# Transposing the second half's x among the first half's products, and keeping its columns in DRAM

## The chip, the cores and the metric

The kernel runs on one core of one Trainium2 chip. The metric is the device time of one execution in microseconds (us), lower is better. The core has five engines that run side by side, each with its own fixed queue of instructions: TensorE (PE, matmuls and transposes; PEld are its weight loads), VectorE (DVE), ScalarE (ACT), GpSimd (POOL) and SyncE (SP, which here only issues DMAs; ACT issues some too).

## The reference, cut to what matters

Two layers over x of 2048 positions by 1024 channels, in float32. Each first forms u from x by a scale and a shift per channel, multiplies u by a wide weight, mixes over time, multiplies by an output weight and normalises:

```python
cond = jax.nn.silu(c)
for l in range(DEPTH):
    shift, scale, gate = ...          # from cond @ ada_w[l] + ada_b[l]
    u = x * (1.0 + scale) + shift
    # l == 0: [a | g | z] = u W_in + b_in; h = a * sigmoid(g); h = causal depthwise conv of 31 taps;
    #         h = swish(LayerNorm(h)); y = (h * silu(z)) W_out + b_out
    # l == 1: [B | C | v | z] = u W_in; y = (B * conv_3(C * v) * silu(z)) W_out
    x = LayerNorm(ALPHA * x + gate * y)
```

## The kernel before

The positions are treated in two halves (`sc` 0 and 1), and each half as its even and odd positions (`hf`). A layer's input product of a half is a list of pairs of 128-column blocks of the weight (12 pairs in layer 0, names `wa`, `wz`). Each pair is computed with seven block products (a seven-product scheme for a 2 by 2 block product) instead of eight, so that seven tiles of u per block of 256 channels are needed: `b11`, `b21`, `t1`, `t2`, `b22`, `t3`, `t4`. Each of them is split in a high part (a cast on ACT) and a low part (a subtraction on POOL or DVE), and one product is 12 matmuls of 128 by 512: high times high, high times low, low times high, for four blocks of channels.

u is needed with channels on the partitions, and x has positions there. `u_block` therefore loads a block of x (`xk`, 128x4x128, two buffers), `u_columns` transposes it on PE into a PSUM bank (`ptx`, tag "tp", two banks that the statistics of the convolution use as well) and applies scale and shift on ACT into a tile `uf` (six buffers). `u_first` and `u_second` then make the seven tiles of one block of channels.

The first half's weights are split as they are used, into five buffers `wa`/`wz`, and each split weight is stored in DRAM (`kepta`, `keptz`, 512 KB each, issued on ACT's queue after the next evacuation) for the second half to load. A weight buffer is free again when its store has landed.

The depthwise convolution of 31 taps runs on DVE (L555, one instruction for each tap; the accumulators are `pca`, `pcb`, `pcd`). It is cut into steps, and `tick` hands out some of them after each product: 3.2 in the body of the first half, 1 in the products listed in `moves`, which are the last eleven of the first half. Among these eleven the generator `second_u` makes the seven u tiles of the second half, in the buffers that the first half's tiles leave.

A scheduler lays out each engine's queue from this program order, from priorities (evacuations and u tiles are urgent, taps are not) and from its own estimate of times. PE's instructions keep the program's order. The names in the profile: `ua0..` and `ua1..` are u tiles of the first and second half, `ufua` is `uf`, `c11`, `c12`, `c22`, `c21` are evacuated products, `pl` the transposes for the statistics.

Of the kernel before, what the change touches and what calls it, by code (L numbers as in the profile page):

```python
# [16 lines left out]
P = 128  # L17
D = 1024
S = 2048
K = D // P  # L20
KH = K // 2
T = 512
# [17 lines left out]
def hybrid_trunk(ctx, tc, x, c, ada_w, ada_b, a_w_in, a_b_in, a_conv_w, a_conv_b,  # L40
# [7 lines left out]
    nc = tc.nc  # L48
# [7 lines left out]
    def st(tag, shape, name, dtype=F32):  # L56
        return sb.tile(shape, dtype, tag=tag, bufs=BUFS[tag], name=name)
# [22 lines left out]
    def store_late(dst, src, then=None):  # L80
        late.append((dst, src, then))
# [30 lines left out]
    def tick(taps, *gens):  # L112
        clock[0] += 1
        due_taps[0] += taps
        conv_steps(int(due_taps[0]))
        due_taps[0] -= int(due_taps[0])
        for gen in gens:
            next(gen, None)
        due = [job for at, job in waiting if at <= clock[0]]
        waiting[:] = [w for w in waiting if w[0] > clock[0]]  # L120
        for job in due:
            job()
# [99 lines left out]
    def u_tile(src, name, eng=None):  # L222
        hi = st("u", [P, T], name + "h", F32R)
        lo = st("u", [P, T], name + "l", F32R)
        split(src, hi, lo, eng)
        return hi, lo
# [12 lines left out]
    def u_block(src, sc, hf, k, su, bu, name, tag):  # L239

        xk = st(tag, [P, NT, P], f"xk{name}{hf}_{k}")
        load(xk, quarters(src)[sc, hf][:, k * P:(k + 1) * P]
             .rearrange("(t p) j -> p t j", p=P), "u")
        return u_columns(xk, hf, k, su, bu, name)
# [6 lines left out]
    def u_second(U, f0, f1, name):  # L251
        (b11, b21), (b12, b22) = f0, f1
        tt = lambda o, a, b: nc.vector.tensor_tensor(o, a, b, op=ALU.subtract)
        with urgent():
            tt(b11, b12, b11)
            U["t1"].append(u_tile(b11, name + "t1", nc.vector))
            U["b22"].append(u_tile(b22, name + "b22"))
            tt(b11, b22, b11)
            U["t2"].append(u_tile(b11, name + "t2"))
            tt(b12, b22, b12)  # L260
            U["t3"].append(u_tile(b12, name + "t3"))
            t4 = st("uf", [P, T], f"{name}t4")
            tt(t4, b21, b11)
            U["t4"].append(u_tile(t4, name + "t4", nc.vector))
# [731 lines left out]
    def slowly(gen, ticks=2):  # L996
        due = 0
        for _ in gen:
            due += ticks
            while due >= 1:  # L1000
                yield
                due -= 1
# [18 lines left out]
    def background_b():  # L1021
# [6 lines left out]
        for h in range(2):  # L1028
            for _ in fold_gate(1, h, b_w_out[0], res[1, 2, h]):
                yield  # L1030
                yield
                yield

    def second_u():

        for i in range(KH):
            f0, f1 = [], []
            for b in range(2):
                for hf, fs in ((0, f0), (1, f1)):
                    fs.append(u_block(x, 1, hf, 2 * i + b, su0, bu0, "ua1", "xk"))  # L1040
                    if hf == 0 or b == 0:
                        yield
            u_parts(US[0, 1], f0, f1, f"ua1{i}")
            yield
# [6 lines left out]
    head = [(0, 6)]  # L1051
    order_a = [at for at in head + order_of(n_a) if at not in early]
    coming = second_u()
    for n, (p, r) in enumerate(order_a):
        product(pa[0][p], r)
        if n < K:
            zero_window(n)
        for n in range(moves.get((p, r), 0)):
            next(coming)
        if (p, r) in ((late_b, 3), (late_a, 4)):  # L1060
            k = 0 if r == 3 else 1
            product(pa[1][0], 1, [k])
            product(pa[1][0], 2, [k])
        queue_convs()
        tick(1 if (p, r) in moves else RATE["a"])
    flush()
    product(pa[1][0], 5, [0, 1])
    product(pa[1][1], 1, [0, 1])
# [130 lines left out]
```

## Time and profile before

| | |
|---|---|
| median of 3 runs | 1720.44 us (1716.67 to 1728.08) |
| the profiled execution, its own time | 1725.78 us |
| its span from first to last instruction | 1724.0 us |
| mean granted TensorE clock | 0.96 of full speed |
| PE busy | 1578.9 us, 92% of the span |
| DVE busy | 1165.1 us, 68% |
| POOL busy | 956.8 us, 56% |
| ACT busy | 665.9 us, 39% |

The shares are means over stages with different limits. The products of layer 0's first half lie between about 105 and 378 us of the span, those of the second half from there to about 615 us.

### The profile page before, as it was taken

The numbers are of one execution on the slowest core, as the hardware profiler recorded it, in microseconds if no ns is written. First come the engines' busy times: TensorE is split into PE (matmuls) and PEld (weight loads), VectorE is DVE, ScalarE is ACT, GpSimd is POOL, SyncE is SP. The second block draws the span as 40 slices with busy tenths as digits, with TensorE's granted clock in tenths as the row PEclk, the third lists the DMA queues.
The fourth block names the chain that finished last, engine by engine and source line by source line (L and its number), as shares of the span: only waits on it lengthen the run. The fifth ranks groups of instructions, "written<-read, shape, count | busy, mean of one in ns | idle before, by whom it ended". The sixth has DMA issues, their size and how long they took to land.

```text
span 1724.0 us, 20944 instructions
## 1 busy us (share of the span) xinstructions
PE 1578.9 (92%) x6860; PEld 1278.1 (74%) x6860; DVE 1165.1 (68%) x1816; ACT 665.9 (39%) x1134; POOL 956.8 (56%) x808
## 2 busy tenths in 40 slices
PE   4699999889999989868999999898899999999996
PEld 3577787668888767656777887677688888878885
DVE  4438999997899887997999963564832222226555
ACT  2345444655533335373444333333732221112221
POOL 4368886965656343866888776727565541121110
PEclk9799999899999989988999999899899999999998
DMA  7358888779999997634777667986688887787995
GB/s 221 114 198 295 293 298 322 228 276 391 333 354 363 357 368 257 208 147 166 265 266 255 245 245 286 342 289 223 220 294 282 306 298 221 229 299 260 329 336 222
DMA packets 237916, 469.64 MB, mean 272 GB/s; under 512 B 20328, under 2 KB 102640, under 8 KB 237808
## 3 DMA queue, kind: packets, MB, share of 16 engines
q1 hardware_dynamic: 190864, 323.06, 55.6%
q10 hardware_dynamic: 46944, 145.25, 21.7%
q8 instruction: 55, 0.90, 0.2%
q14 instruction: 53, 0.43, 0.1%
HBM read 297.72 MB, written 170.52 MB: 272 GB/s over the span
## 4 chain that ended last, share of the span: by engine, by line
PE 59%; DVE 18%; DMA 11%; issue 4%; POOL 3%; ACT 3%; SPq 1%; ACTq 0%; DVEq 0%; POOLq 0%
PE po L98 17%; PE pxb L98 7%; PE pxc L98 7%; PE pxa L98 5%; PE pzb L98 4%; DVE pca L555 4%; PE pzc L98 4%; PE pza L98 3%; DVE pcb L555 3%; DMA keptb<-wb 3%; PE pxz L98 2%; DMA wr<-w_dram 2%; DMA kepta<-wa 2%; PE pya L98 2%; PE pyb L98 2%
## 5 line engine op out<-in xcount | busy, mean ns | idle before, releaser
L555 DVE SCALAR_TENSOR_TENSOR pcb<-h,w,pcb 128x512 f32<-128x512 f32 x224 | 166.7, 744 | 8.4 <-ACT pcb L563 8.0
L555 DVE SCALAR_TENSOR_TENSOR pca<-h,w,pca 128x512 f32<-128x512 f32 x192 | 142.8, 744 | 0.2
L555 DVE SCALAR_TENSOR_TENSOR pca<-xs,w,pca 128x512 f32<-128x512 f32 x128 | 95.5, 746 | 0.8
L825 DVE TENSOR_TENSOR r<-po,r 128x512 f32<-128x512 f32 x64 | 43.3, 683 | 70.0 <-PE po L98 31.6
L555 DVE SCALAR_TENSOR_TENSOR pcd<-xs,w,pcd 128x512 f32<-128x512 f32 x112 | 83.4, 745 | 0.1
L500 POOL TENSOR_TENSOR ada<-ada,adaw 128x512 f32<-128x512 f32 x48 | 63.9, 1331 | 35.1 <-ACT adaw L494 16.0
L795 ACT ACTIVATE r<-r,nb,rs 128x512 f32<-128x512 f32 x64 | 47.3, 808 | 80.4 <-DVE nb L792 80.3
L220 POOL TENSOR_TENSOR gb_0l<-vb,gb_0h 128x512 fp32r<-128x512 f32 x4 | 5.2, 1295 | 110.2 <-ACT gb_0h L219 110.2
L530 POOL TENSOR_TENSOR wf<-wf,grow 128x512 f32<-128x512 f32 x32 | 41.9, 1318 | 37.6 <-DMA wf<-in_b_w_out_dram 33.6
L832 POOL TENSOR_TENSOR rs<-rs,mhalf 128x1 f32<-128x1 f32 x32 | 18.3, 584 | 75.6 <-DVE rs L831 75.6
L220 POOL TENSOR_TENSOR wa<-rawa,wa 128x512 fp32r<-128x512 f32 x32 | 43.2, 1352 | 21.2 <-ACT wa L219 21.0
L569 POOL TENSOR_TENSOR lead<-lead,part 128x512 f32<-128x512 f32 x32 | 43.6, 1362 | 19.8 <-ACT part L568 17.3
L220 POOL TENSOR_TENSOR wc<-rawc,wc 128x512 fp32r<-128x512 f32 x32 | 46.0, 1437 | 15.5 <-ACT wc L219 15.3
L894 POOL TENSOR_TENSOR hb1c<-c12c,c22c 128x512 f32<-128x512 f32 x16 | 21.1, 1322 | 59.1 <-DVE c22c L392 54.8
L220 POOL TENSOR_TENSOR wf<-wf 128x512 fp32r<-128x512 f32 x32 | 43.0, 1351 | 18.4 <-ACT wf L219 13.7
L804 DVE TENSOR_TENSOR r<-r,g 128x512 f32<-128x512 f32 x48 | 39.6, 838 | 20.0 <-PE ptx L101 17.5
L786 POOL TENSOR_TENSOR r<-r,gb 128x512 f32<-128x512 f32 x32 | 43.9, 1388 | 15.7 <-DMA r<-in_x_dram 14.4
L817 ACT ACTIVATE ub<-ptx,post_sh,post_sc 128x128 f32<-128x128 f32 x128 | 47.0, 482 | 13.4 <-PE ptx L101 13.4
L494 ACT ACTIVATE adaw<-adaw,cond 128x512 f32<-128x512 f32 x64 | 42.5, 715 | 24.8 <-DMA adaw<-in_ada_w_dram 24.3
L220 POOL TENSOR_TENSOR wb<-rawb,wb 128x512 fp32r<-128x512 f32 x32 | 45.2, 1412 | 7.6 <-ACT wb L219 7.4
L220 POOL TENSOR_TENSOR wb<-sb,wb 128x512 fp32r<-128x512 f32 x24 | 35.4, 1473 | 25.0 <-ACT wb L219 25.0
L739 ACT ACTIVATE v<-v,second_columns 128x512 f32<-128x512 f32 x32 | 25.9, 814 | 55.0 <-DVE v L738 53.8
(1388 smaller groups left out, 5589.2 us busy)
## 6 DMA issues: line engine op xcount, KB each, us to landing
wr<-w_dram SPq DMA_DIRECT2D x128, 512.0 KB
kepta<-wa ACTq DMA_DIRECT2D x56, 512.0 KB
wa<-kepta SPq DMA_DIRECT2D x56, 512.0 KB
keptc<-wc ACTq DMA_DIRECT2D x56, 512.0 KB
keptb<-wb ACTq DMA_DIRECT2D x56, 512.0 KB
wc<-keptc SPq DMA_DIRECT2D x56, 512.0 KB
wb<-keptb SPq DMA_DIRECT2D x56, 512.0 KB
adaw<-in_ada_w_dram SPq DMA_DIRECT2D x32, 512.0 KB
```

What stands on the lines that cost most here:

```text
L98: return tc.keep_in_program_order(nc.tensor.matmul(*args, **kw))
L220: (eng or nc.gpsimd).tensor_tensor(lo, src, hi.bitcast(F32), op=ALU.subtract)
L494: nc.scalar.activation(raw[:, j], raw[:, j], AF.Identity, scale=cond[:, kk + j:kk + j + 1])
L500: nc.gpsimd.tensor_tensor(acc, acc, raw[:, j], op=ALU.add)
L530: nc.gpsimd.tensor_tensor(w[:, 1], w[:, 1], grow, op=ALU.mult)
L555: nc.vector.scalar_tensor_tensor(out=tiles[out], in0=src, scalar=w, in1=tiles[acc], op0=ALU.mult, op1=op)
L569: nc.gpsimd.tensor_tensor(lead, lead, part, op=ALU.add)
L786: nc.gpsimd.tensor_tensor(rt, rt, gb[0][h], op=ALU.add)
L795: nc.scalar.activation(rts[t, h], rts[t, h], AF.Identity, scale=rs, bias=nb)
L804: eng.tensor_tensor(r, r, g[h], op=ALU.mult)
L817: nc.scalar.activation(fs[k][:, t * P:(t + 1) * P], pt[:, j * P:(j + 1) * P], AF.Identity, scale=post_sc[:, k:k + 1], bias=post_sh[:, k:k ...
L825: nc.vector.tensor_tensor(r, pss[t], r, op=ALU.add)
```

## The change

The sixteen blocks of the second half's x are loaded, transposed, scaled and shifted early, one block after every fourth product of the first half (`columns_early`), and each resulting tile is stored in DRAM (`ux_dram`, 256 KB, on ACT's queue). `second_u` then loads these tiles (`ux`) instead of making them. In the eleven products of `moves` no steps of the convolution are handed out any more, where there was one for each. The low part of `t2` is computed on DVE instead of POOL for the second half.

```diff
-            U["t2"].append(u_tile(b11, name + "t2"))
+            U["t2"].append(u_tile(b11, name + "t2", nc.gpsimd if name < "ua1" else nc.vector))
...
+    ux_dram = dt_([2, K, P, T], "ux_dram")
+
+    def columns_early():
+
+        for k in range(K):
+            for hf in range(2):
+                f = u_block(x, 1, hf, k, su0, bu0, "ua1", "xk")
+                store_late(ux_dram[hf, k], f)
+                yield
+
     def second_u():
...
-                    fs.append(u_block(x, 1, hf, 2 * i + b, su0, bu0, "ua1", "xk"))
+                    k = 2 * i + b
+                    f = st("uf", [P, T], f"ux{hf}_{k}")
+                    load(f, ux_dram[hf, k], "u")
+                    fs.append(f)
...
+    transposed = slowly(columns_early(), 4)
...
-        tick(1 if (p, r) in moves else RATE["a"])
+        tick(0 if (p, r) in moves else RATE["a"], transposed)
```

On PE, where the last product of one pair (`pzz`) is followed by the first of the next (`pxa`), before:

```order
L98 MATMUL pzz_0_2035<-ua03b22h,wz_0_3_2109 128x512
L98 MATMUL pzz_0_2035<-ua03b22l,wz_0_3_2109 128x512
L98 MATMUL pzz_0_2035<-ua03b22h,wz_0_3_2109 128x512
L98 MATMUL pxa_0_2130<-ua00b11h,wa_0_1_2134 128x512
L98 MATMUL pxa_0_2130<-ua00b11l,wa_0_1_2134 128x512
```

and now:

```order
L98 MATMUL pzz_0_2175<-ua03b22h,wz_0_3_2250 128x512
L98 MATMUL pzz_0_2175<-ua03b22l,wz_0_3_2250 128x512
L98 MATMUL pzz_0_2175<-ua03b22h,wz_0_3_2250 128x512
L101 MATMUL ptxua_7_2273<-ident,xkua_7_2271 128x128 x4
L98 MATMUL pxa_0_2280<-ua00b11h,wa_0_1_2284 128x512
L98 MATMUL pxa_0_2280<-ua00b11l,wa_0_1_2284 128x512
```

Four transposes of a block of the second half's x have moved in between; there are sixteen such places, 49 or 50 rows apart, and all of them now stand before the eleven products of `moves`.

At the same place on ACT, which evacuates, casts weights and issues the stores, before:

```order
L693 ACTIVATE c12z_0_2101<-c12z_0_2101 128x512
L88 DMA keptz_0_1941<-wz_0_3_2109 128x1024
L387 ACTIVATE c11a_0_2149<-pxa_0_2130,half_b 128x512
L88 DMA z_dram<-c12z_0_2101 128x512
L88 DMA kepta_0_2131<-wa_0_1_2134 128x1024
```

and now:

```order
L236 ACTIVATE ufua_7_2278<-ptxua_7_2273,mod_106 128x512
L693 ACTIVATE c12z_0_2242<-c12z_0_2242 128x512
L88 DMA keptz_0_2071<-wz_0_3_2250 128x1024
L219 CAST wa_0_5_2371<-sa_0_2369 128x512
L387 ACTIVATE c11a_0_2299<-pxa_0_2280,half_b 128x512
L88 DMA z_dram<-c12z_0_2242 128x512
L88 DMA ux_dram<-ufua_7_2278 128x512
L88 DMA kepta_0_2281<-wa_0_1_2284 128x1024
```

The scale and shift of the block and its store have come in, the store ahead of a store of a weight.

On DVE, near the end of the making of the second half's u, from the low part of the last `t1` on, before:

```order
L220 TENSOR_TENSOR ua13t1l<-ufua_6_2899,ua13t1h 128x512
L555 SCALAR_TENSOR_TENSOR pcb_5_3235<-h_5_3232,w_87,pcb_5_3235 128x512
L555 SCALAR_TENSOR_TENSOR pca_5_3234<-h_5_3232,w_87,pca_5_3234 128x512
L253 TENSOR_TENSOR ufua_6_2899<-ufua_7_2952,ufua_6_2899 128x512
L394 SCALAR_TENSOR_TENSOR c11a_1_3022<-pya_1_2771,c11a_1_3022 128x512
L587 SCALAR_TENSOR_TENSOR acc_5_3486<-pca_5_3234,second_columns,pt_5_3459 128x512
L593 SCALAR_TENSOR_TENSOR pca_5_3234<-pca_5_3234,negb,pt_5_3459 128x512
L253 TENSOR_TENSOR ua13t_2981<-ufua_7_2943,ufua_6_2899 128x512
```

and now:

```order
L220 TENSOR_TENSOR ua13t1l<-ux_6_2960,ua13t1h 128x512
L555 SCALAR_TENSOR_TENSOR pcb_5_3348<-h_5_3345,w_87,pcb_5_3348 128x512
L555 SCALAR_TENSOR_TENSOR pca_5_3347<-h_5_3345,w_87,pca_5_3347 128x512
L253 TENSOR_TENSOR ux_6_2960<-ux_7_2991,ux_6_2960 128x512
L555 SCALAR_TENSOR_TENSOR pcb_5_3348<-h_5_3345,w_87,pcb_5_3348 128x512
L555 SCALAR_TENSOR_TENSOR pca_5_3347<-h_5_3345,w_87,pca_5_3347 128x512
L253 TENSOR_TENSOR ua13t_3020<-ux_7_2989,ux_6_2960 128x512
L220 TENSOR_TENSOR ua13t2l<-ux_6_2960,ua13t2h 128x512
L587 SCALAR_TENSOR_TENSOR acc_5_3603<-pca_5_3347,second_columns,pt_5_3598 128x512
L593 SCALAR_TENSOR_TENSOR pca_5_3347<-pca_5_3347,negb,pt_5_3598 128x512
```

The low part `ua13t2l` has come in, and the taps stand among the u steps as they did. Counted from the queue's start, 237 taps stand ahead of the last `t2` (the L253 row after `ua13t1l`) in the order before, and 237 ahead of `ua13t2l` now. Counted from the last gate (L679, `c21a`) of the pair that is third from the end, they are 56 of 94 instructions before and 48 of 89 now: eight taps have moved from this stretch to places before it.

## Rows read from the trace of the kernel before

**Rows 1.** Windows view, three stretches: busy us (instructions) per engine, granted clock, DMA share, GB/s

```profile
core 0: us, PE busy (x) PEld busy (x) DVE busy (x) ACT busy (x) POOL busy (x), PEclk, DMA share, GB/s
160.00:300.00 140.00, 135.69 (x603) 109.74 (x601) 132.79 (x210) 69.05 (x114) 110.46 (x92) 1.00 0.85 305
301.00:378.00 77.00, 62.98 (x268) 50.08 (x268) 74.00 (x106) 46.32 (x78) 57.46 (x45) 0.89 0.70 235
380.00:530.00 150.00, 150.00 (x686) 124.01 (x685) 131.93 (x215) 74.01 (x118) 92.92 (x76) 1.00 0.98 363
```

**Rows 2.** The chain that ended last, 275 to 378 us: start, us, what

```profile
275.55 2.73 PE pza L98 x12
...
278.73 6.60 DMA kepta<-wa
...
285.36 0.63 ACT wa L219
...
286.06 1.30 POOL wa L220
...
290.03 6.34 DMA kepta<-wa
...
311.99 6.24 DMA xkua<-in_x_dram
...
323.37 0.69 DVE c12a L394
...
367.19 0.60 DVE ufua L253
...
376.73 1.29 POOL ua13t2l L220
```

**Rows 3.** Timeline of DVE, 301 to 373 us: start, us, what [idle before <-releaser]

```profile
301.71 1.02 DVE L679 SCALAR_TENSOR_TENSOR c21a<-c21a,c11a 128x512 f32<-128x512 f32 x1
...
304.73 0.69 DVE L394 SCALAR_TENSOR_TENSOR c11a<-pya,c11a 128x512 f32<-128x512 f32 x1 [0.67 <-PE pya L98]
...
315.39 0.75 DVE L555 SCALAR_TENSOR_TENSOR pcb<-h,w,pcb 128x512 f32<-128x512 f32 x1
316.05 0.75 DVE L555 SCALAR_TENSOR_TENSOR pca<-h,w,pca 128x512 f32<-128x512 f32 x1
316.71 1.69 DVE L220 TENSOR_TENSOR ua10t1l<-ufua,ua10t1h 128x512 fp32r<-128x512 f32 x1
...
348.45 0.68 DVE L220 TENSOR_TENSOR ua11t4l<-ua11t,ua11t4h 128x512 fp32r<-128x512 f32 x1
...
372.64 0.68 DVE L253 TENSOR_TENSOR ufua<-ufua,ufua 128x512 f32<-128x512 f32 x1
```

**Rows 4.** Timeline of PE, same stretch

```profile
318.37 0.63 PE L101 MATMUL ptxua<-ident,xkua 128*128 128x128 f32 x4 [2.12 <-DMA xkua<-in_x_dram]
...
326.79 0.60 PE L101 MATMUL ptxua<-ident,xkua 128*128 128x128 f32 x4
327.14 0.48 PE L98 MATMUL pxz<-ua00t2h,wz 128*128 128x512 f32 x1
...
378.06 0.50 PE L98 MATMUL pxa<-ua13t2l,wa 128*128 128x512 f32 x1 [0.78 <-POOL ua13t2l L220]
```

**Rows 5.** DMA queues, 105 to 300 us: packets, MB, share of 16 engines

```profile
q10 hardware_dynamic: 13198, 41.75, 55.1%
q1 hardware_dynamic: 24364, 15.81, 27.4%
```

**Rows 6.** Waits, 150 to 300 us: us in total, times, longest

```profile
ACT wa L219 <- DMA kepta<-wa: 20.8, 13, 4.8
```

**Rows 7.** Timeline of POOL, 316 to 324 us

```profile
316.59 1.26 POOL L220 TENSOR_TENSOR wz<-sz,wz 128x512 fp32r<-128x512 f32 x1
...
322.68 1.28 POOL L220 TENSOR_TENSOR ua10t2l<-ufua,ua10t2h 128x512 fp32r<-128x512 f32 x1
```

**Rows 8.** Windows view, a stretch in layer 1's first products, columns as in Rows 1

```profile
860.00:900.00 40.00, 39.09 (x175) 31.70 (x175) 40.00 (x64) 16.68 (x29) 32.51 (x30) 1.00 0.75 264
```

**Rows 9.** Waits of SP's DMA queue, 301 to 378 us

```profile
SPq L71 <- PE ptxua L101: 33.8, 12, 11.9
```

## The prediction

> **What bounds the kernel now.** I read the windows view first, because the change touches one place: the products of layer 0's first half and the passage to the second. Three stretches are to be seen in [rows 1]. In the first half's products (160 to 300 us) PE is busy 135.69 of 140 us and DVE 132.79: both are nearly full, and the DMA share is 0.85. In the passage, where the second half's u is made (301 to 378), PE falls to 62.98 of 77 at a granted clock of 0.89, and DVE is busy 74.00 of 77. After it (380 to 530) PE is busy throughout, 150.00 of 150, at a DMA share of 0.98, and DVE has 18 us to spare.
>
> The chain [rows 2] says what ends last in each. In the first half it is now and then the landing of a stored weight (`kepta` or `keptz`; seven pieces between 118 and 297 us, the last two shown, 6.60 and 6.34 us), since a weight buffer is reused only then. At 311.99 it is the load of a block of x, for which PE stood at the transposes (2.12 us, [rows 4]). From 323.37 to 367.8, however, nearly every piece is an instruction of DVE, one behind the other, and most of these are convolution taps. The last step is POOL's low part `ua13t2l`, for which PE waits until 378.06. So the passage is bound by DVE's queue, with PE's waits for x mostly beside it. That decides how I cost the change.
>
> **Part by part.** *Transposes.* Four transposes hold PE for 0.35 us (326.79 to 327.14, [rows 4]). Sixteen such blocks are 5.6 us, which leave the passage, where PE has spare time, and enter the first half's products, where it has 4.3 us of idle in 140 [rows 1]. So the cost is 5.6 us if none of that idle takes them, and 1.3 us if all of it does. I take 5.6, as PE runs without a gap for long stretches there. ACT's sixteen activations go the same way and are hidden: ACT is busy 69.05 of 140 us.
>
> *DMA.* The sixteen loads of x move into the first half, and sixteen stores of 256 KB come with them; the passage gets sixteen loads of 256 KB instead. SP's and POOL's queues lose and gain nothing else, but each xk load now stands on SP among the loads of raw weights, and each store on ACT ahead of a weight's store. From [rows 5], SP's queue q1, which carries x, spent 0.274 x 195 x 16 / 24364 = 0.035 us for a packet; a block of x comes in 512 pieces (128 partitions by 4), so 1.1 us of all 16 engines. The store, at q10's rate (41.75 MB in 0.551 x 195 us), is 0.67 us. Together 1.8 us for each block, and 13 blocks in 160 to 300 us bring the share from 0.85 to about 0.98 of a stretch that is 4.6 us longer. On average it fits. What it costs lies between nothing, as in the 150 us after the passage, where PE was full at a share of 0.98 [rows 1], and 1.8 us on each of the chain's seven landings, 12.6 us. I take 2 us: the full stretch is the nearer row in share, but there weights are loaded ahead, while here the buffers wait for stores (20.8 us of ACT's waits, [rows 6]). The Trainium skill says in "DMA: Bandwidth & Descriptors", section "Issuing engines are not separate DMA queues", that DMAs issued by different engines run on the same 16 engines and interleave. It speaks against the change, as a store of columns and a load of x then both delay a weight's store; the upper bound of 12.6 us is the sum by that.
>
> *The passage on DVE.* The change takes eleven taps from the program's text there, but not from the queue. The order shows 237 taps ahead of the last `t2` before and 237 ahead of its low part now. Taps wait in a backlog that DVE carries into the passage, and the scheduler fills with them what it is given. What changes is that eight of them now stand before the passage, in the first half, where DVE gets the 5.6 us by which PE is longer (8 x 0.66 = 5.3 us; 0.66 us from tap to tap at 315.39 and 316.05, [rows 3]). That leaves the start of the passage 7.6 us later (5.6 + 2), at 309.3 instead of 301.71.
>
> From there DVE had 94 instructions to the last `t2` (301.71 to 373.32, 71.6 us [rows 3]), of which 2.6 us were waits (three, the first shown: 0.67 for PE). I drop them, as they hung on PE behind its x blocks: 69.0. Eight taps less: 63.7. The four low parts of `t2` that come from POOL cost between 0.68 us (348.45) and 1.69 us (316.71) each on DVE [rows 3]; I take the middle, 1.2, so +4.8. One subtraction of 0.68 less is in the stretch, as the last one is now behind it. Sum 67.8 us. The passage ends for PE with `ua13t2l` at 309.3 + 67.8 = 377.1, where it was 378.06. The 4.7 us from 373.32 to 378.06, in which the last `t2` waited for ACT and POOL [rows 2], go, since DVE makes the low part itself.
>
> Why a split on DVE costs so much more at one time than at another is to be seen in [rows 3, 7]: the one of 1.69 us began 0.12 us after a subtraction on POOL, and ended 0.55 us after that one's end; the one of 0.68 us met none. The Trainium skill gives the rule in "SBUF — State Buffer", section "SBUF: two separate sides": a DVE instruction with two SBUF inputs and a GpSimd instruction that reads SBUF hold a port pair exclusively, and the loser blocks for the whole instruction. The trace agrees. By it, moving these splits to DVE is dear wherever POOL is busy: four at 1.69 would make the sum 2 us longer. It gives POOL back 4 x 1.28 us [rows 7], which no one waits for except at the very end.
>
> *Afterwards.* Eleven taps (7.3 us of DVE) come later than their products did. The next 150 us have 18 us of DVE to spare [rows 1], and they run on, as a backlog, to the end of the convolution about 1000 us. In between DVE is full in places (40.00 of 40 at 860 us) with PE at 39.09 [rows 8]. I cost this at nothing, with PE as the cover; without it, it would be up to 7.3 us. A queue that is laid out anew everywhere after the change may move the rest by some 4 us either way (the three runs before differ by 11).
>
> **The sum.** +5.6 +2 in the first half, and 67.8 instead of 76.35 (301.71 to 378.06) in the passage, -8.5: together -0.9 us. The profiled execution took 1725.78 us (span 1724.0 and 1.8 around it), so 1724.9 by its own time; it lay 5.3 above the median of the three runs, which carries over: 1720.44 - 0.9 = **1719.5 us**. Differences within 1% (17.2 us) are about what a measurement of this kernel can't tell from none.
>
> **The rivals.** *Stores hold the weights (slower).* The place is the five weight buffers of the first half. A buffer's round is a cast on ACT (0.63 us) and a subtraction on POOL (1.30), up to one product (2.73) until the store is issued, and a landing of up to 6.60 [rows 2]: 11.3 us, against five products, 13.6. So from a landing of about 9 us on PE waits for every buffer. For it: ACT's 13 waits [rows 6] and a share going to 0.98. Against it: even the longest landing leaves 2.3 us, and an added block is 1.8. If each of the seven landings is longer by one block the sum is +5.6 +12.6 -8.5, 1730; if the sixteen blocks all count, 16 x 1.8 = 28.8 us, 1746.
>
> *DVE isn't the bound (faster).* If POOL's subtractions miss those on DVE, 41 instructions at 0.68 and 48 taps at 0.66 make 59.6 us, and PE's idle takes the transposes: +1.3 - 16.7, 1705. PE itself could do it: without the 64 transposes of x it has 204 instructions in the passage, 45 us at the pace after it (150 us for 686, [rows 1]). Against it is that POOL is busy 57.46 of 77 us [rows 1] and that four more such instructions come to DVE.
>
> *The loads of columns come late (a new wait in place of the old).* SP stood 33.8 us behind PE's transposes in the passage [rows 9]; now it stands behind the six `uf` buffers, four of which a block's loads need, and a landing lies between a buffer's release and the first subtraction, where there was an activation. A load of x took 6.24 us on the chain [rows 2], and the order leaves 8 to 19 instructions (5.6 us at the least) between two blocks. If each of the three later blocks is 2 us late, DVE loses 6: 1725.5. For it is that DVE has taps to fill only as far as the fixed order allows; against it, that 2 KB rows land faster than x's 512-byte pieces by the two prices above.
>
> **How the numbers follow.** The forecast (no change, 1711 to 1727) 0.55; stores 0.17; DVE not the bound 0.13; late loads 0.15. The range of 1704 to 1734 takes in the lower end of the second rival and the price of seven landings with a late block or two. Over 1% faster needs the whole of the second rival and some luck afterwards: 0.09. Over 1% slower needs more than seven landings' price: 0.08. Within 1%: 0.83.
>
> **What would show it.** In the changed profile: stretch 160 to 300 at a DMA share near 0.98 with PE's idle not above 6 us; the `c21a` that began at 301.71 now near 309; DVE busy over 95% until `ua13t2l`, with taps among the u steps; PE's first matmul on `ua13t2l` near 377; no wait for `xkua` in the passage. I am wrong if that matmul comes before 370 (DVE was not the bound, or lost its stretching) or after 384 (weights or columns waited), or if the time comes or goes after 400 us.

## The result, and the profile after

The kernel with the change takes 1742.64 us (median of 4 runs, 1736.96 to 1748.53), the kernel before in the same rounds 1720.78 (4 runs, 1716.67 to 1728.08): a ratio of 1.0117, 95% interval 1.0080 to 1.0153. It is some 20 us slower, where no change was forecast and the range ended at 1734. The profiled execution took 1736.96 us (span 1735.2), the lowest of its runs, while that of before lay above its median. So I compare two profiles of each: the first ones, and one more of each kernel, unaltered (the first two experiments; spans 1719.7 of before, 1739.6 of the change). By these four profiles the change costs 15.5 us; what the other runs lose beyond that can't be placed.

The windows view after, for the stretches of [rows 1, 8]:

```profile
core 0: us, PE busy (x) PEld busy (x) DVE busy (x) ACT busy (x) POOL busy (x), PEclk, DMA share, GB/s
160.00:300.00 140.00, 137.72 (x632) 111.46 (x631) 133.37 (x213) 74.52 (x122) 112.58 (x91) 1.00 0.93 331
301.00:378.00 77.00, 59.48 (x210) 44.94 (x209) 74.30 (x106) 36.59 (x62) 57.61 (x43) 0.84 0.66 240
380.00:530.00 150.00, 147.78 (x676) 121.92 (x676) 116.85 (x195) 73.10 (x116) 88.99 (x71) 1.00 0.99 358
860.00:900.00 40.00, 38.72 (x172) 31.11 (x171) 39.43 (x61) 15.78 (x27) 32.07 (x29) 1.00 0.72 256
```

In the first half PE's idle has gone from 4.3 to 2.3 us, and the DMA share is 0.93 (forecast near 0.98). In the passage PE has 58 instructions fewer, and yet DVE is as full as it was. The timeline of DVE at the two ends of the passage, after [rows 3]:

```profile
310.97 0.97 DVE L679 SCALAR_TENSOR_TENSOR c21a<-c21a,c11a 128x512 f32<-128x512 f32 x1
...
377.07 0.68 DVE L220 TENSOR_TENSOR ua13t2l<-ux,ua13t2h 128x512 fp32r<-128x512 f32 x1
```

Here the forecast (309.3 and 377.1) holds to 2 us. But PE was not there yet. Its timeline in the passage, every wait of 0.8 us or more up to the last product of the first half, and the first matmul on `ua13t2l` [rows 4]:

```profile
315.05 0.47 PE L98 MATMUL pza<-ua00t1h,wa 128*128 128x512 f32 x1 [1.93 <-DVE c11a L394]
324.34 0.50 PE L98 MATMUL pza<-ua00b22h,wa 128*128 128x512 f32 x1 [1.97 <-ACT wa L219]
326.40 0.79 PE L98 MATMUL pza<-ua00b22h,wa 128*128 128x512 f32 x1 [1.33 <-POOL wa L220]
343.60 0.79 PE L98 MATMUL pzz<-ua00b22h,wz 128*128 128x512 f32 x1 [5.59 <-ACT wz L219]
353.02 0.80 PE L98 MATMUL pya<-ua10b21h,wa 128*128 128x512 f32 x1 [2.70 <-DVE c12z L392]
367.15 0.50 PE L98 MATMUL pxz<-ua00t4h,wz 128*128 128x512 f32 x1 [2.10 <-ACT wz L219]
369.21 0.51 PE L98 MATMUL pxz<-ua00t4h,wz 128*128 128x512 f32 x1 [1.33 <-POOL wz L220]
...
385.01 0.39 PE L98 MATMUL pxa<-ua13t2l,wa 128*128 128x512 f32 x1
```

The last products of the first half (`t4h`) came at 367 to 372 us, and PE used `ua13t2l` at 385.01, eight microseconds after it was begun. It waited for the last split weights of the first half (`wa`, `wz`) and for evacuations. Before, its longer waits there had been for `xkua`, for a scaled block and for split weights; three that [rows 4] do not show:

```profile
333.24 0.50 PE L98 MATMUL pzz<-ua00b22h,wz 128*128 128x512 f32 x1 [2.19 <-POOL wz L220]
...
338.48 0.63 PE L101 MATMUL ptxua<-ident,xkua 128*128 128x128 f32 x4 [2.23 <-DMA xkua<-in_x_dram]
...
360.24 1.97 PE L101 MATMUL ptxua<-ident,xkua 128*128 128x128 f32 x8 [2.36 <-ACT ufua L236]
```

The wait of 5.59 us is read back in the timelines of POOL and then ACT after:

```profile
338.27 1.72 POOL L220 TENSOR_TENSOR ua11b22l<-ux,ua11b22h 128x512 fp32r<-128x512 f32 x1
339.96 1.25 POOL L348 TENSOR_TENSOR sz<-rawz,sz 128x512 f32<-128x512 f32 x1
```

```profile
338.89 0.62 ACT L219 CAST ua11t2h<-ux 128x512 fp32r<-128x512 f32 x1 [0.17 <-DVE ux L253]
...
341.79 0.62 ACT L219 CAST ua11t4h<-ua11t 128x512 fp32r<-128x512 f32 x1 [0.99 <-DVE ua11t L253]
...
342.94 0.60 ACT L219 CAST wz<-sz 128x512 fp32r<-128x512 f32 x1
```

The sum `sz` stood on POOL behind low parts of u, and the cast `wz` on ACT behind casts of u, one of which waited for DVE.

**Where the time went.** The product matmuls (L98 on PE) have the same order in all kernels, so the start of the same matmul can be compared. Three places cut the span into four parts: the matmuls that stood at 292.5, 395.0 and 1516.0 us in the first profile of before. Means of the two profiles of each kernel, us:

| part | before | after | difference | forecast |
|---|---|---|---|---|
| to the place at 292.5 | 292.9 | 301.8 | +8.9 | +7.6 |
| passage, 300 matmuls to 395.0 | 100.8 (102.4, 99.2) | 103.9 (102.3, 105.4) | +3.1 | -8.5 |
| on to 1516.0 | 1119.5 | 1124.3 | +4.9 | 0 |
| to the end | 208.7 | 207.4 | -1.3 | 0 |
| span | 1721.8 | 1737.4 | +15.5 | -0.9 |

The first line is nearly as forecast. The passage is wrong by 11.6 us, the other lines together by some 5. The +3.1 us by itself is no more than what two profiles of one kernel differ by; that the 8.5 us did not come is clear of it.

### The profile page after: what moved, and what is told of

It reads as the page before. It is cut to its first block, busy times and chain, and to the rows that moved or that the text cites. A ratio compares the mean times of both kernels' runs of the same rounds, so it can differ in the third digit from the quotient of the medians.

```text
span 1735.2 us, 21033 instructions
## 1 busy us (share of the span) xinstructions
PE 1582.6 (91%) x6860; PEld 1275.6 (74%) x6860; DVE 1160.7 (67%) x1820; ACT 666.1 (38%) x1134; POOL 951.9 (55%) x804
## 4 chain that ended last, share of the span: by engine, by line
PE 55%; DVE 12%; DMA 7%; POOL 6%; issue 5%; ACT 3%; SPq 0%; ACTq 0%; POOLq 0%; DVEq 0%
PE po L98 15%; PE pxb L98 7%; PE pxc L98 7%; PE pxa L98 5%; PE pzb L98 4%; PE pxz L98 3%; PE pzc L98 3%; PE pza L98 3%; DVE pca L555 2%; PE pyb L98 2%; PE pzz L98 2%; DMA keptb<-wb 2%; PE pyc L98 1%; PE pya L98 1%; DMA wr<-w_dram 1%
## 5 line engine op out<-in xcount | busy, mean ns | idle before, releaser
L739 ACT ACTIVATE v<-v,second_columns 128x512 f32<-128x512 f32 x32 | 25.9, 815 | 65.9 <-DVE v L738 64.0
```

## The experiments

The runs of a group shared a chip and the runs of the kernel before; ratios are against these, with their 95% interval. "Behind at 395" is the start of the matmul that stood at 395.0 us in the first profile of before, against that profile; "passage" is the time of the 300 matmuls up to it.

**The two kernels again.** Expected of the changed kernel:

> The changed kernel once more, unaltered, for its spread and a second profile. If its loss against the kernel before (20 us by the medians, 11 by the two profiles) is the early part's cost plus a passage that gave nothing back, the second profile again has PE some 8 us late at the first products after the passage (near 400 us), and whatever else is lost comes later. If the loss is an accident of one profile, the places differ.

and of the kernel before:

> The kernel before once more, unaltered, for a second profile: the first lay 4 us above the median of its runs. If PE's places agree with the first profile to within 2 us up to 600 us, the differences found there are the kernels' and not one execution's.

The change: 1740.94 us, 1.0093 (1.0056 to 1.0129), 13.1 us behind at 395. The kernel before, one run: 1721.54 us, 2.5 us ahead there. So two profiles of one kernel differ by some 3 us in the length of the passage and by up to 5 in the place at its end, more than the 2 us that were expected, and less than that is not read as an effect below.

**The early transposes and stores alone**, with `second_u` and the taps as before:

```diff
+                f = u_block(x, 1, hf, k, su0, bu0, "ue", "xk")
+                store_late(ux_dram[hf, k], f)
...
-        tick(1 if (p, r) in moves else RATE["a"])
+        tick(1 if (p, r) in moves else RATE["a"], transposed)
```

> The kernel before with the early transposes and their stores added and never loaded: the second half's u is made as before, so the transposes are done twice. Theory one (the early part costs about 8 us and the passage gives nothing back): PE is 8 to 9 us late at 300 us, as in the changed kernel, the passage takes what it took before, the time is 8 to 10 us over the kernel before. Theory two (the new passage itself costs the time): less than 4 us over. A rival by stores that hold the weights: over 12 us.

1747.02 us, 1.0124 (1.0086 to 1.0163). The profiled execution (1735.75) was the lowest; in it PE is 8.5 us behind at 292.5, which confirms that line of the sum. The rest of the expectation was missed: the passage, whose text is that of the kernel before, takes 106.0 us where that kernel took 102.4 and 99.2, and by the ratio the kernel is some 21 us over it, not 8 to 10. So the early part may cost something in the passage as well; no run separates that.

**The loads alone**, without the early transposes and stores:

```diff
-                    load(f, ux_dram[hf, k], "u")
+                    load(f, quarters(x)[1, hf][k % NT * P:(k % NT + 1) * P, k // NT * T:(k // NT + 1) * T], "u")
...
-        tick(0 if (p, r) in moves else RATE["a"], transposed)
+        tick(0 if (p, r) in moves else RATE["a"])
```

> The changed kernel without the early part: the second half's u is made of plain rows of x loaded at the same places in pieces of the same size, so the transposes, scale and shift of the second half are left out. It is the passage of the changed kernel alone. Theory one (DVE's queue with its taps bounds the passage, so loads in place of transposes give little): PE is at the first products after the passage between 3 us earlier and 1 us later than in the kernel before, and the time is within 5 us of it. Had the passage been bound by PE's transposes and waits for x, it would be 8 to 16 us faster. If columns that come late cost the time: 4 to 8 us slower.

1745.01 us, 1.0124 (1.0099 to 1.0149). No time is lost in the first half (0.7 us), and still the passage is not shorter: 109.0 us, with DVE busy 98.80 of them. Even with nothing paid for it, taking the transposes out of the passage gains nothing; it is 7 to 10 us longer. Nor is the kernel as a whole faster than the changed one: it is level with the kernel before at the place of 612.7 us (0.1 us behind its first profile) and loses 18 us from there on. So the first half's loss can't simply be taken off the total. The run differs from the changed kernel in one thing more, the plain rows of x that it loads; the run without the stores, which loads them too, has 108.4.

**One step of the convolution after each product of `moves`, as before:**

```diff
-        tick(0 if (p, r) in moves else RATE["a"], transposed)
+        tick(1 if (p, r) in moves else RATE["a"], transposed)
```

> The changed kernel with one step of the convolution handed out after each of the eleven products, as before. The order of DVE has the same 233 taps ahead of the last low part of t1 and 238 ahead of the last of t4 with and without. Theory: the passage doesn't change (within 1 us at 400 us); what can change is later, where the eleven taps come earlier again: 0 to 8 us faster than the changed kernel. If the edit did what it says, the passage would be 5 to 8 us longer.

1741.55 us, 1.0102 (1.0083 to 1.0121), the same as the change; passage 102.6. The edit of the taps is worth nothing here.

**No steps in the last 22 products of the first half**, which does take taps off DVE's queue (20 between the first `t1` and the last `t4`, where there were 48):

```diff
+    held_back = order_a[-22:]
...
-        tick(0 if (p, r) in moves else RATE["a"], transposed)
+        tick(0 if (p, r) in held_back else RATE["a"], transposed)
```

> The changed kernel with no steps of the convolution handed out in the last 22 products of the first half, so that the backlog runs dry: the order has 21 taps between the last gate of the third-last pair and the last low part of t1, where there are 44. Theory one (taps in DVE's queue delay the u steps, ACT's casts of weights stand behind the casts of u, and PE waits for weights): PE's waits for ACT and POOL weights and for c12z in the passage, 13 to 19 us together, shrink by half, and PE is 6 to 14 us earlier near 400 us than in the changed kernel; some of it is lost again where the taps come later. Theory two (late loads of columns through the uf buffers): less than 3 us.

1746.06 us, 1.0155 (1.0136 to 1.0175). Passage 98.1: DVE is busy only 66 us of it, and the passage is 4 to 7 us shorter than with the change. It is paid for at the end of the half's products. The timeline of PE there:

```profile
631.56 0.66 PE L101 MATMUL pl<-ident,acc 128*128 128x128 f32 x2 [13.71 <-DVE v L737]
```

The first output needs the finished convolution, and waits for the held taps.

**One more `uf` buffer** (one `xk` buffer less):

```diff
-BUFS = dict(u=56, raw=4, s=1, w=5, ta=8, hin=1, xk=2, xs=1, pt=1, acc=3, tv=2, uf=6)
+BUFS = dict(u=56, raw=4, s=1, w=5, ta=8, hin=1, xk=1, xs=1, pt=1, acc=3, tv=2, uf=7)
```

> The changed kernel with seven uf buffers and one xk buffer. Theory two (a block's loads wait for buffers that the block before still uses, and what follows comes late): the passage is 3 to 8 us shorter. Theory one (taps): within 2 us of the changed kernel at 400 us. One xk buffer may cost up to 2 us in the first half.

1746.01 us, 1.0149 (1.0123 to 1.0174), passage 103.2. The loads of columns, for which SP waited in the changed kernel (the waits of SP's queue, 301 to 378 us: in total, times, longest; [rows 9]), are not what holds PE:

```profile
SPq L71 <- DVE ux L253: 34.4, 3, 12.1
```

With the seventh buffer this wait is 23.7 us, and the passage is as long as it was.

**Without the stores** (the loads take plain rows of x):

```diff
-                store_late(ux_dram[hf, k], f)
...
-                    load(f, ux_dram[hf, k], "u")
+                    load(f, quarters(x)[1, hf][k % NT * P:(k % NT + 1) * P, k // NT * T:(k // NT + 1) * T], "u")
```

> The changed kernel without the sixteen stores of columns; the second half's u is made of plain rows of x, loaded as the columns were (so the second half's u is left wrong). It prices the stores in the first half. If PE's lateness of 8 to 10 us at 300 us is the transposes alone (5.6) plus their place on ACT and PE, it stays at 6 or more; if the stores delay the weights' stores, it falls to 5 to 6.

1741.77 us, 1.0132 (1.0110 to 1.0153). PE is 8.0 us behind at 292.5, with the stores 8.4 and 10.1. The other kernels that have the early part with its stores lie between 7.5 and 12.3 there, so what the stores cost by that place can't be told from nothing. The passage takes 108.4 us, with plain rows of x loaded as in the loads alone (109.0).

**`t2`'s low part on POOL, as before:**

```diff
-            U["t2"].append(u_tile(b11, name + "t2", nc.gpsimd if name < "ua1" else nc.vector))
+            U["t2"].append(u_tile(b11, name + "t2", nc.gpsimd))
```

> The changed kernel with the low part of t2 back on POOL; transposes, stores, loads and taps as changed. If DVE's queue is what ends the passage, four splits of about 1.2 us leave it, and PE, which was 8 to 13 us behind the first profile of before at the product that stood at 395 us there, is 4 to 5 us less behind (+4 to +8). If the last split weights of the half are what PE waits for, POOL gets four instructions of 1.28 us that stand among the sums and splits of these weights, and PE is as late as with the change or later (+9 to +15). The whole: within 5 us of the changed kernel by either, 1737 to 1746.

1742.68 us, 1.0128 (1.0096 to 1.0159); 7.8 us behind at 395, passage 102.0. DVE is relieved (87 us busy against 90) and PE gets nothing of it: this edit is worth nothing either.

**The kernel before with the taps held:**

```diff
+    held_back = order_a[-22:]
...
-        tick(1 if (p, r) in moves else RATE["a"])
+        tick(0 if (p, r) in held_back else RATE["a"])
```

> The kernel before with no steps of the convolution handed out in the last 22 products of the first half (it handed out 3.2 or 1 after each); nothing else is changed, so x is still transposed in the passage. In the order some 31 taps less stand on DVE up to the last t2, 31 x 0.66 = 20 us. If DVE alone is the bound of the passage before, PE is 12 us or more ahead of the first profile of before at 395 us. If the passage is bound by a mesh of waits in which x, the last split weights and DVE take turns, it is 3 to 7 us ahead. By both the taps come back after 600 us, where the kernel with the change and these taps held lost 15 us: so the whole is 1725 to 1738, above the kernel before.

1738.70 us, 1.0093 (1.0065 to 1.0122). This decides on the prediction's reading: with 31 taps less DVE is busy 65.9 of 98.1 us, and PE is 3.3 us ahead at 395, an unaltered run 2.5. The passage of the kernel before did not hang on DVE's sum of work. The loss of 15.9 us after 612 us is the same as above (a wait of 13.44 us for `v` at 623.60).

**Weights first**: in the last 14 products the weights' sums, casts and low parts get a higher priority than all else.

```diff
...
-                split(src, wt[:, 0], wt[:, 1])
+                with weights(): split(src, wt[:, 0], wt[:, 1])
...
```

The same is put around each sum of two blocks of a weight.

> The changed kernel in which, in the last 14 products of the first half, the sums, casts and low parts of the weights go ahead of everything else on ACT and POOL that is ready (a higher priority for the scheduler). If PE waits in the passage for the last split weights because they are queued behind the u tiles and the convolution on ACT and POOL, its waits for wz and wa there (5.59, 2.10, 1.97, 1.33, 1.33 us in the changed kernel) shrink to under 5 us together, and PE is 4 to 8 us less behind at 395 us (+1 to +6 against the first profile of before). If they hang on something else (stores that must land, DVE's queue behind the sums), the lateness stays at +8 to +13. The whole follows by as much, 1733 to 1738 by the first, 1741 by the second.

1753.27 us, 1.0184 (1.0161 to 1.0207), 14.4 us behind, passage 107.0. The waits for `wz` and `wa` get less (the two near 342 us are 2.41 and 1.21, with one of 3.22 ahead of them). Two others grow and make up for it: 5.83 us for DVE's evacuation `c12z`, where there was 2.70, and 4.34 for ACT's `c11a` at 388.64, where there was 1.04. The first of them on PE:

```profile
354.75 0.79 PE L98 MATMUL pya<-ua10b21h,wa 128*128 128x512 f32 x1 [5.83 <-DVE c12z L392]
```

My theory that the order on ACT and POOL alone was the cause falls: the wait moved.

**Weights first, and the taps held:**

> As the run before it (weights first), and no steps of the convolution in the last 22 products as well. If weights and DVE's taps are two separate parts of the wait, the gains add: PE is no later at 395 us than 1 us behind the first profile of before, to 5 us ahead. If they are one chain, it is where the better of the two alone is (+2 to +4). After 600 us the held taps come back as they did without the weights first (some 15 us), so the whole is 1740 to 1746 whatever happens in the passage; if it is under 1735, the loss after 600 us was not owed to the held taps.

1743.83 us, 1.0129 (1.0108 to 1.0151). 4.8 us behind at 395, passage 95.1, the shortest of all, 7 to 10 us less than after; 16 us are lost after 612 us.

**POOL relieved.** POOL is busy 38.42 of 44 us from 301 to 345 after, 39.95 before. Four kernels tell whether it is the bound. The changed kernel with the taps held and all low parts of the second half's u on DVE:

```diff
-        split(src, hi, lo, eng)
+        split(src, hi, lo, nc.vector if name[:3] == "ua1" else eng)
```

> The changed kernel with no convolution steps in the last 22 products (as in the run that held the taps) and all 28 low parts of the second half's u on DVE, so that sixteen leave POOL (16 x 1.28 to 1.75 = 20 to 28 us). POOL is busy 38 to 42 of 44 us in 301 to 345 in every kernel so far. If POOL's queue bounds the first part of the passage, the weights' sums and splits come sooner: the 5.01 us wait for wz near 342 is under 2, and PE is 4 us or more ahead of the run that held the taps at 395 us, at -1 or earlier against the first profile of before (+3.2 there). If the passage hangs on DVE's u steps, fourteen more of 0.68 to 1.7 us make it 5 to 12 us later than there (+8 to +15). After 600 us the held taps cost some 15 us by either.

1744.84 us, 1.0156 (1.0120 to 1.0192); 3.4 us behind, passage 97.4, as with the taps held alone. The changed kernel with the sums of the last two pairs' weights on DVE (`adds` set to `nc.vector`):

> The changed kernel in which only the sums of the weights of the last two pairs of layer 0 (four each, 1.28 us on POOL) are made on DVE. If POOL bounds the passage and each sum stands in the chain to a split weight, the chain is 8 x 0.5 us shorter and POOL has 10 us less: waits for wa and wz in the passage shrink from 12 to under 7 us, and PE is 3 to 8 us less late at 395 us (0 to +5, against +8 to +13). If DVE bounds, eight more instructions of 0.7 us make it 5 us later (+13 to +18); if the two take turns, it stays at +8 to +13.

1737.74 us, 1.0108 (1.0082 to 1.0133); 6.7 us behind, passage 100.3, 2 to 5 us less than after, with DVE at 97.33 of 100.34. The kernel before with the low parts on DVE:

> The kernel before with all 28 low parts of the second half's u on DVE, taps as before. The order has 97 DVE instructions between the first t1 and the last t4 where there were 84. If DVE bounded the passage (the reading in the prediction), PE is 9 to 15 us later at 395 us than the first profile of before. If POOL bounded its first part and DVE only the end, the two cancel in part: 0 to +7.

1732.13 us, 1.0080 (1.0050 to 1.0110); 4.6 us behind, passage 106.5, DVE 99.77 of it. And with the taps held as well:

> The kernel before with those low parts on DVE and the taps held in the last 22 products, 64 DVE instructions in the same stretch. The run with the taps held alone (45 instructions) was 3.3 us ahead at 395 us, and so was an unaltered run (2.5). If POOL bounds the passage, this one is 6 to 12 us ahead of the first profile of before at 395; if DVE bounds, it is later than the run with the taps held alone by up to 13 us (+0 to +10); if neither (x, the stored weights' landings and the buffers), it is within 2 us of -3.

1740.48 us, 1.0118 (1.0088 to 1.0148); 2.3 us ahead, passage 98.6. The windows view of this last one, over the 300 matmuls:

```profile
294.05:392.68 98.63, 83.61 (x366) 66.48 (x364) 71.42 (x99) 56.17 (x93) 45.09 (x36) 0.93 0.77 276
```

DVE, POOL and ACT all have a quarter to a half of the time to spare, and PE still idles 15 us. So the load of none of the three sets the passage by itself. More work on DVE lengthened it in one run (99.8 us of it: 106.5) and not in another (the sums on DVE, 97.3: 100.3); 20 to 28 us less shortened it by 2 to 9 us against the mean of two profiles.

**Transposes put back.** What is left is what the transposes themselves did. Sixteen groups of four transposes of the identity, which nobody reads, where the blocks of x were transposed, and then twice as many:

```diff
                     load(f, ux_dram[hf, k], "u")
                     fs.append(f)
+                    pt = bank("tp", f"pfill{hf}_{k}")
+                    for t in range(NT):
+                        transpose(pt[:, t * P:(t + 1) * P], ident, ident)
```

> The changed kernel with sixteen groups of four transposes of the identity, read by nobody, put on PE where the kernel before transposed the blocks of x. Between the product matmuls that stood at 292.5 and 395.0 us in the first profile of before (the same 300 matmuls in every kernel) that kernel spent 102.4 us: 16.0 idle, 9.7 in transposes, 76.7 in matmuls; the changed one 102.3 and in a second run 105.4: 19.7 and 22.7 idle, 1.3 and 0.9 in transposes, 81.3 and 81.9 in matmuls. If the transposes had only filled time in which PE waited for u, weights and evacuations, and kept its clock up, this kernel takes 101 to 106 us there: 13 to 17 idle, 9 to 10 in transposes, 74 to 78 in matmuls. If PE's own work set the length of the passage, it takes 108 to 111. The whole stays at 1738 to 1744 by the first, 1746 to 1750 by the second.

> The same with twice as many transposes (eight for each block of x, 17 us of PE in all). If something other than PE paces the passage, it is still 102 to 108 us long there, with idle down to 7 to 13 and matmuls at 73 to 77, since part of these transposes falls where PE isn't waiting. If PE's own work paces it: 114 to 118.

1736.08 us, 1.0095 (1.0064 to 1.0126), and 1743.28, 1.0132 (1.0091 to 1.0174). Both lengths of the passage are near the first reading of the expectations (100.1 us for 101 to 106, 103.7 for 102 to 108). The windows view over the same 300 matmuls of the passage, columns as above, of the first profile of before, then after, then once and twice as many transposes put back.:

```profile
292.54:394.97 102.43, 86.42 (x374) 69.17 (x372) 94.01 (x132) 60.65 (x100) 76.43 (x60) 0.92 0.78 275
```

```profile
300.89:403.24 102.35, 82.61 (x310) 63.48 (x309) 90.02 (x129) 50.79 (x84) 74.61 (x56) 0.88 0.75 276
```

```profile
301.97:402.07 100.10, 86.02 (x374) 67.36 (x372) 91.82 (x128) 49.11 (x82) 71.83 (x54) 0.93 0.74 271
```

```profile
302.46:406.16 103.70, 91.72 (x438) 73.71 (x436) 91.06 (x129) 50.58 (x84) 75.72 (x56) 0.93 0.74 270
```

Split by the view of the lines (L98 are the product matmuls, L101 the transposes, idle is the length less PE's busy time; time in which both are under way counts in both columns, while the expectation above counted it once):

| kernel | passage | L101 busy | L98 busy | PE idle | granted clock |
|---|---|---|---|---|---|
| before, two profiles | 102.4, 99.2 | 11.3, 11.2 | 79.7, 77.1 | 16.0, 15.6 | 0.92, 0.95 |
| after, two profiles | 102.3, 105.4 | 1.7, 1.2 | 81.9, 82.4 | 19.7, 22.7 | 0.88, 0.85 |
| transposes put back | 100.1 | 10.6 | 79.2 | 14.1 | 0.93 |
| twice as many | 103.7 | 17.8 | 77.9 | 12.0 | 0.93 |

Sixty-four transposes more or less change nothing in the length of the passage that is clear of its spread: they take the place of idle time. In the kernel before they were free. All twenty profiles agree on the length: in the eight with transposes of x or of the identity it is 98.1 to 106.5 us (mean 101.8), in the twelve without 95.1 to 109.0 (102.6). The idle time is 12.0 to 20.7 us (15.8) with them and 17.7 to 25.5 (21.4) without. The time of the 300 matmuls and the clock only lean the same way and overlap: 76.7 to 80.4 us (78.4) and 0.87 to 0.95 with them, 76.4 to 83.6 (80.8) and 0.85 to 0.95 without. As a whole the kernel with the transposes put back (1.0095) isn't told from the change (1.0117 and 1.0093).

## Why the prediction was wrong

**The step that failed** is the one on the passage: "The passage ends for PE with `ua13t2l` at 309.3 + 67.8 = 377.1, where it was 378.06", from which it booked 8.5 us. DVE's part of it came out (66.8 us from the start of `c21a` to the end of `ua13t2l`, forecast 67.8), but PE's time did not hang on it: it came to that matmul at 385.01, 7.3 us after DVE had made the tile (in the second profile at 391.28, 10.7 us after). The sign of being wrong that the prediction named ("after 384", weights or columns waited) is what was seen, by the weights. The chain of waits named DVE piece after piece, and I took its sum for the length of the passage. PE's own waits said otherwise, in a row on which the prediction itself rested: for `ua13t2l` it waited 0.78 us [rows 4], so 0.78 us was all that an earlier `ua13t2l` could give at that place. PE's own way through the passage ended 0.78 us ahead of it; begun 8.4 us later, as in the first profile after, and otherwise as long, it would end at 378.06 - 0.78 + 8.4 = 385.7, near the 385.01 measured (by the second profile 387.4, and 391.28 measured). In no profile of the changed kernel or of its variants did PE wait for `ua13t2l` at all. Its longer waits before were for blocks of x (2.12 and 2.23 us), split weights (1.94 and 2.19), a weight loaded back (2.02) and a scaled block (2.36). The run of the kernel before with the taps held shows it: 28 us less on DVE, 1 to 4 us less in the passage.

**What took its place.** The transposes and the waits for x filled time in which PE had to wait anyway. Without them PE's idle grew by 5.4 us (means of two), and the same 300 matmuls took 3.7 us longer, at a mean granted clock of 0.88 and 0.85 where it had been 0.92 and 0.95. Matmuls and transposes overlap, so PE's busy time as a whole fell by only 2.3 us, and the passage did not become shorter (+3.1 us, within the spread). Putting transposes back brings both figures back; but two kernels without transposes there took 79.5 us for the 300 matmuls (`t2` on POOL, taps held) and one 76.4 (weights first and taps held), so the slower matmuls don't follow from the missing transposes alone. That transposes left a place "where PE has spare time" stands in the prediction, and it booked nothing for their leaving; that was right. What it booked there was DVE's time.

**What paces the passage stays open in part.** It isn't the load of DVE, POOL or ACT alone, nor a buffer of columns, nor the order of the weights alone; of the kernels above none went under 95 us. The traces show waits that change hands: relieve one queue, and PE waits for the next (`wz` 5.59 to 2.41, `c12z` 2.70 to 5.83). I read that as a chain across queues that are each worked in order, where a cast of a weight stands behind a cast of u that waits for DVE. The run with the weights first cut one link, and the wait moved; with the taps held as well the passage is the shortest of all (95.1 us, one profile). No run cut the whole chain, so it is argued and not shown.

**The first half** (+5.6 and +2) was right in kind and short by 1.3 us: 8.9. The run with the loads alone, without the early part, lost 0.7 us there, so the early part is the cause; by the run without stores most of it is the transposes and their loads (8.0), which the prediction had at 5.6 and a part of the 2. ACT's waits for stored weights, the place of the slower rival, hardly grew (150 to 300 us; all four kinds together 31.7 us before and 33.5 after). The largest of them, 20.8 us in [rows 6], reads after:

```profile
ACT wa L219 <- DMA kepta<-wa: 20.6, 13, 4.2
```

But one place was missed. The timelines of ACT and PE after, at the second block:

```profile
117.58 2.60 ACTq L88 DMA_DIRECT2D kepta<-wa  x2
120.23 0.78 ACT L236 ACTIVATE ufua<-ptxua,mod 128x512 f32<-128x512 f32 x1 [2.49 <-issue]
120.90 0.61 ACT L219 CAST wa<-sa 128x512 fp32r<-128x512 f32 x1
```

```profile
121.56 0.50 PE L98 MATMUL pxa<-ua00t2h,wa 128*128 128x512 f32 x1 [1.26 <-ACT wa L219]
```

Between 98 and 124 us 3.8 us are lost: two stores' issues and the new activation stand ahead of a cast for which PE waits. In the kernel before, that cast was begun at 116.31. Without the stores of columns PE is only 0.7 us behind at that place; that kernel came as late by other losses before 292.5.

**The edits priced on DVE.** `t2`'s low part on DVE was booked at 4.8 us and taps outside the passage at 5.3; both edits undone leave the time where it was. They were sums on a queue that wasn't the bound.

**Afterwards** was booked at nothing, up to 7.3 us without cover. From the place at 395.0 to that at 612.7 the change gains 6 us (217.7 and 217.0 before, 211.4 and 211.0 after), from there to 697.6 it loses 7 (85.0 and 85.4; 91.6 and 93.4): I read it as the taps that come back where the first output needs the convolution, 1.2 us in sum. The run with the taps restored has neither the gain nor most of the loss (216.5 and 87.1), and is no faster. From 697.6 to 1516.0 3.7 us more are lost. The kernels above differ there between 815 and 832 us, also where their text is the same after the passage, so I take it for the effect of a queue laid out anew, which the prediction put at some 4 us; no run isolates it.

**The rivals.** The time came out on the side of the slower ones, to which over 1% slower had been given 0.08, but not by their mechanisms. "DVE isn't the bound" was right in its premise and wrong in its result, since PE wasn't free to go on. "Late loads" were there (the 34.4 us of SP) and cost nothing that another buffer would give back. The stores held the weights hardly longer than before. That the transposes had been free, so that the change could only cost, was the rival that I lacked, and it ends where the kernel does.

None of the sixteen altered kernels beats the kernel before; the nearest is that kernel with its low parts on DVE, at 1.0080.

## What to carry to other kernels

Price a stage by the waits of the engine that you want to speed up, one by one and by what ended each, and not by the sum of the queue that the chain of waits names most: a queue that is full, but ends 0.78 us late for the one who needs it, has 0.78 us to give at that place. Work that fills such waits is free where it is, and moving it to a place where the engine is full costs its whole length or more (here 8 to 9 us for 5.6 us of transposes, with their loads). Where an engine stalls on several queues in turn, take work from one and look which wait grows, before counting the gain.

## What the runs showed of the hardware

After most of PE's longer waits in the passage the granted clock stood at the lower of its two levels, 1.2 instead of 2.4 GHz, for some microseconds. In the changed kernel, after the wait of 5.59 us, it was 0.50 from 343.60 to 346.00 us. Most matmuls there began 0.43 us apart, where others begin 0.23 us apart, and the twelve of that product took 5.79 us (343.60 to 349.39), against 2.73 at the full clock [rows 2]. The Trainium skill advises in "TensorE: Matmul & The Clock Gate", section "Why this matters for your kernels", against leaving PE idle between bursts of matmuls; these rows agree.

The mean granted clock of the passage is a mix of the two levels. Of the kernel before it was 0.92 and 0.95, of the changed kernel 0.88 and 0.85, and with transposes of no use put back 0.93 in both runs. But it was 0.87 in the run with the early part alone, which has the transposes, and 0.95 in the run with the weights first and the taps held, which has none. So transposes put back, with nothing else changed, went with a higher clock in two profiles against two; by the spread over the other kernels that is a leaning and not a rule.
